# A two-layer transformer trunk on one core: the third gate/up chunk takes its K pairs in the later chunks' order, and a hold on two weight rests is taken out

## The chip, the cores and the metric

The kernel runs on one core of one Trainium2 chip. The metric is device time in microseconds (us), less is better. Before the change three runs took 2182.69, 2183.49 and 2186.39; the median is 2183.49.

## What is computed

Two layers, 256 tokens, model width 2048, feed-forward width 5632, all in float32:

```python
def reference(x, ...):
    for l in range(DEPTH):                                  # DEPTH = 2
        h = rms_norm(x, pre_mix_norm[l])
        m = hybrid_mixer(h, l, w_in[l], w_o[l], ...)        # two kinds of attention
        x = x + rms_norm(m, post_mix_norm[l])
        h = rms_norm(x, pre_ffn_norm[l])
        f = swiglu(h, w_gate[l], w_up[l], w_down[l])
        x = x + rms_norm(f, post_ffn_norm[l])
    return x

def swiglu(h, w_gate, w_up, w_down):
    return (jax.nn.silu(h @ w_gate) * (h @ w_up)) @ w_down
```

The change touches `h @ w_gate` and `h @ w_up` alone.

## The kernel before

**Products in three.** Each float32 weight tile is split in two: `hi` is a rounded copy that ScalarE (ACT) makes (L310), and `lo`, the rest, is the tile minus `hi`, mostly made by VectorE (DVE, L320), in a few cases by GpSimd (POOL, L313). The tokens are split likewise. A product is then three matmuls on TensorE (PE): hi x hi, hi x lo, lo x hi.

**Chunks and pairs.** The gate/up phase of a layer has 11 chunks of 512 columns, c = 0 to 10. A chunk takes the 2048 rows of K in 8 pairs of 256, kp = 0 to 7. Each pair brings two tiles of 128 x 1024 values: one of `w_gate`, one of `w_up`. Tiles are numbered in the order in which the program takes them, and names carry these numbers. In layer 1, pair (1, 6) is tiles 156 and 157, (1, 7) is 158 and 159, (2, 0) is 160 and 161. The next two pairs of chunk 2 are 162 to 165. Later (3, 5) is 186 and 187, (3, 6) is 188 and 189, (3, 7) is 190 and 191, and (4, 0) is 192 and 193.

**Plain and seven-product pairs.** A plain pair (`eight`, matmuls at L1255) is 24 matmuls. A seven-product pair forms seven products in place of eight blocks (Strassen's way), 21 matmuls (`seven_products`, its three at L1137, L1138 and L1139). It needs sums of weight blocks. The up tile, called T, comes with a second DMA by POOL that adds the gate tile's first half on the way (L259); the gate tile is called G. `mixed_weights` then has DVE subtract within T (L291), add that to G (L292), and form three rests behind ACT's copies (L280, L282): `lo`, `Tl` of 512 values, `Tl` of 1024 values. PE wants these in the order lo, Tl 512, Tl 1024. Token sums for it are made once in chunks 0 to 2 (`pair_sums`).

Chunk 1 has seven-product pairs kp = 5 and 6; chunk 2 has 2, 4, 5 and 6; chunks 3 to 9 (`MORE_AT`) have 2, 3, 4, 5 and 6. Chunk 2 takes its pairs as 0, 1, 2, ... 7; chunks 3 to 9 take them as 0, 2, 1, 3, ... 7 (`MORE_ORDER`), so that a seven-product pair is second.

**Buffers.** The plain tiles (`raw`) have 4 buffers, `hi` 6, `lo` 6, G 3, T 4. Weights lie in DRAM in the order of use. SyncE (SP) issues their loads in one queue, first in, first out (raw L242, G L231, T L258): a load whose buffer isn't free yet holds up all that stand behind it.

**Who sets the order.** Most instructions are placed by a scheduler in the compiler that goes by its own times and by dependencies that the program adds. Three of those matter here. After a chunk's last seven-product pair DVE adds up the shared products (`shared_part`, L1179 to L1182). If the next chunk's second pair is a seven-product pair, that pair's rests are made to come behind these (`follows`); if not, the next plain rest that the program asks for is held behind them (`held`). And the POOL's rest of the second pair's gate tile waits for the newest seven-product matmul (`helped`). Finally `last_of_row` names the up tile of pair (1, 6) in each layer: the two plain rests that come after it, those of pair (1, 7), are held behind its last Tl.

**A chunk's end.** With the last pair the chunk before last is transposed on PE (L1372), and ACT copies the result out of PSUM (L1373), two copies; the next chunk's sums go into the banks that they free. DVE and ACT then drain the finished chunk's banks (L1433 to L1439), and its seven-product pairs' banks are in turn those of the next chunk but one.

Of the kernel before, what the change touches and what calls it, by code (L numbers as in the profile page):

```python
# [45 lines left out]
NEXT_SEVEN = (5, 6)  # L46
MORE_SEVEN = (2, 3, 4, 5, 6)
MORE_AT = (3, 4, 5, 6, 7, 8, 9)
# [24 lines left out]

def gate_order(c):

    if c in MORE_AT:
        return MORE_ORDER
    return FIRST_ORDER if c == 0 else tuple(range(KT // 2))


def weight_order():

    order = []

    def queue_pair(name, l, kp, c):
        order.append((name, l, kp, c))
        return len(order) - 1

    plan = []
    sevens, plain, own = set(), set(), set()  # L90
    for l in range(L):
        lay = {"in": {}, "o": {}, "gate": {}, "up": {}, "down": {}}
        for n, (ca, cb) in enumerate(PAIRS):
            for kp in IN_ORDER if n else range(KT // 2):
                lay["in"][ca, kp] = queue_pair("w_in", l, kp, ca)
                lay["in"][cb, kp] = queue_pair("w_in", l, kp, cb)
                if kp in IN_NOW[n]:
                    plain.add(lay["in"][cb, kp])
        order_o = [(c, kp) for kp in KP_O for c in (0, 1)]
        order_o += [(c, kp) for kp in LATE_O for c in (2, 3)] + [(c, kp) for c in (2, 3) for kp in LAST_O]  # L100
        lay["order_o"] = order_o
        for c, kp in order_o:
            lay["o"][c, kp] = queue_pair("w_o", l, kp, c)
            if c == 3 and kp in O_SEVEN:
                own.add(lay["o"][c, kp])
        for c in range(FF // CW):
            for kp in gate_order(c):
                lay["gate"][c, kp] = queue_pair("w_gate", l, kp, c)
                lay["up"][c, kp] = queue_pair("w_up", l, kp, c)
                if kp in gate_sevens(c):  # L110
                    sevens.add(lay["up"][c, kp])
        for half in range(2):
            for kp in range(FF // P // 2):
                for c in (2 * half, 2 * half + 1):
                    lay["down"][c, kp] = queue_pair("w_down", l, kp, c)
                if kp in DOWN_SEVEN[half]:
                    sevens.add(lay["down"][2 * half + 1, kp])
        plan.append(lay)
    return order, plan, sevens, plain, own
# [48 lines left out]
def kernel(  # L168
# [35 lines left out]
    order, plan, sevens, plain, own = weight_order()  # L204
# [3 lines left out]
    for lay in plan:  # L208
        for c in range(1, FF // CW):
            for n in (1, 2):  # L210
                helped[lay["gate"][c, gate_order(c)[n]]] = n == 1
    newest_seven = [None]
    last_of_row = {lay["up"][1, NEXT_SEVEN[-1]] for lay in plan}

    ready = {}
    raws, loads = [], []
# [47 lines left out]
    def mixed_weights(i):  # L264

        g, u = raws[i - 1], raws[i]
        hi = wpool.tile([P, 2, CW], F32R, tag="hi", bufs=6, name=f"hi{i}")
        lo = wpool.tile([P, 2, CW], F32R, tag="lo", bufs=6, name=f"lo{i}")
        if i in own:
            th = wpool.tile([P, 2, CW], F32R, tag="hi", bufs=6, name=f"Th{i}")  # L270
            tl = wpool.tile([P, 2, CW], F32R, tag="lo", bufs=6, name=f"Tl{i}")
            th2 = mix_pool[0].tile([P, 2 * (S + P)], F32R, tag="ah", bufs=1, name=f"T2h{i}")[:, 0:CW]
            tl2 = mix_pool[0].tile([P, 2 * (S + P)], F32R, tag="al", bufs=1, name=f"T2l{i}")[:, 0:CW]
        else:
            th = mix_pool[0].tile([P, 3, CW], F32R, tag="Th", bufs=1 if i in plain else 2, name=f"Th{i}")
            tl = mix_pool[0].tile([P, 3, CW], F32R, tag="Tl", bufs=1 if i in plain else 2, name=f"Tl{i}")
            th2, tl2 = th[:, 2, :], tl[:, 2, :]

        def split(h, l, w):
            nc.scalar.activation(h, w, AF.Copy)  # L280
            with in_row(i):
                newest_rest[i] = nc.vector.tensor_tensor(out=l, in0=w, in1=h.bitcast(F32), op=ALU.subtract)  # L282

        if i in plain or i in own:
            with after_rests():
                nc.vector.tensor_tensor(out=u[:, 0, :], in0=g[:, 0, :], in1=u[:, 0, :], op=ALU.add)
        split(hi, lo, u)
        t1, b22 = ((hi[:, k, :], lo[:, k, :]) for k in range(2))
        t3, t4 = ((th[:, k, :], tl[:, k, :]) for k in range(2))
        t2 = u[:, 1, :]  # L290
        nc.vector.tensor_tensor(out=t2, in0=t2, in1=u[:, 0, :], op=ALU.subtract)  # L291
        nc.vector.tensor_tensor(out=g, in0=g, in1=t2.unsqueeze(1).to_broadcast([P, 2, CW]), op=ALU.add)  # L292
        split(th2, tl2, t2)
        split(th[:, 0:2, :], tl[:, 0:2, :], g)
        if i in last_of_row:
            held[:] = newest_rest[i], 2
        t2 = th2, tl2
        return {"b22": b22, "t1": t1, "t2": t2, "t3": t3, "t4": t4}

    def feed(upto):  # L300
        fetch(upto)
        while fed[0] < min(upto, len(stream)):
            i = fed[0]
            raw = raws[i]
            if i in sevens or i in plain or i in own:
                ready[i] = mixed_weights(i)
                fed[0] += 1
                continue
            hi = wpool.tile([P, 2, CW], F32R, tag="hi", bufs=6, name=f"hi{i}")
            nc.scalar.activation(hi, raw, AF.Copy)  # L310
            lo = wpool.tile([P, 2, CW], F32R, tag="lo", bufs=6, name=f"lo{i}")
            if i in helped:
                rest = nc.gpsimd.tensor_tensor(out=lo, in0=raw, in1=hi.bitcast(F32), op=ALU.subtract)  # L313
                if helped[i]:
                    tc.add_manual_dep(rest.ins, newest_seven[0].ins.name, AFTER, reason="the shared port")
                ready[i] = (hi, lo)
                fed[0] += 1
                continue
            with behind():
                rest = nc.vector.tensor_tensor(out=lo, in0=raw, in1=hi.bitcast(F32), op=ALU.subtract)  # L320
            ready[i] = (hi, lo)
            fed[0] += 1
            rests.append(rest)
# [21 lines left out]
    held = [None, 0]  # L345
    follows, newest_rest = {}, {}

    def in_row(i):

        return tc.issue_after(follows[i].ins) if i in follows else nullcontext()  # L350
# [8 lines left out]
    def after_rests():  # L359

        return tc.issue_after(rests[-1].ins)
# [826 lines left out]
    for l in range(L):  # L1188
# [27 lines left out]
        for kp in LATE_O[:-1]:  # L1216
            i, j = (plan[l]["o"][c, kp] for c in (2, 3))
# [44 lines left out]
        with tc.manual_schedule(engines=by_hand):  # L1262
# [35 lines left out]
            fetch(fed[0] + 4)  # L1298
            first_banks = four_banks(1, [f"c{q}_{l}_0" for q in ("11", "12", "21", "22")])
            first, second, third, fourth = gate_order(0)[:4]  # L1300
            eight(first_banks, 0, first, (0,), True, False, ahead=0)
            eight(first_banks, 0, second, (0,), False, False, (0,), 0)
# [302 lines left out]
```

## Time and profile before

| | |
|---|---|
| runs, us | 2182.69, 2183.49, 2186.39 (median 2183.49) |
| profiled execution | 2185.51 us, span 2183.8 |
| PE busy | 2168.2 us, 99% |
| DVE busy | 1912.0 us, 88% |
| ACT busy | 1392.1 us, 64% |
| POOL busy | 256.1 us, 12% |
| PE's clock | full in all slices |
| weights from DRAM | 215 GB/s over the span |
| gate/up chunk 2, layer 1 | 482.88 to 527.32 us |
| gate/up chunks 3 to 9, layer 1 | 527.32 to 815.96 us |
| the same in layer 2 | 1569.90 to 1612.32, and to 1902.80 us |

Times in rows of a time line are from the start of the span: start, length, engine, line, operation, tile written <- tiles read, shape; in brackets how long the engine was idle before it and what ended that. Consecutive rows of one kind are merged (x4 is four of them). In the waits view the numbers behind the colon are us in total, times, and the longest.

### The profile page before, as it was taken

To read this page: it belongs to the slowest core of one execution; us is meant where nothing else is said; L and a number is where in the kernel's file an instruction comes from. 1 tells how busy PE (TensorE), PEld (TensorE's weight loads), DVE (VectorE), ACT (ScalarE), POOL (GpSimd) and SP (SyncE) were. 2 spreads that over 40 slices of the span, in tenths; PEclk is the share of its full clock that TensorE was granted. 3 is DMA by queue.
4 is the path that set the end of the run, shared out by engine and by line. 5 is a ranking of instruction groups with operands and counts; after the bars stand their busy time and mean duration, and the time that the engine had idled before them with its cause. 6 is when DMAs were issued, how large, how long until landed. Compare 5 with 4: busy or idle time off the path is not lost.

```text
span 2183.8 us, 28775 instructions
## 1 busy us (share of the span) xinstructions
PE 2168.2 (99%) x9956; PEld 1783.6 (82%) x9956; DVE 1912.0 (88%) x2641; ACT 1392.1 (64%) x2081; POOL 256.1 (12%) x239
## 2 busy tenths in 40 slices
PE   9999999999999999999999999999999999999998
PEld 7888888887888888888878888888888888888886
DVE  7888658889999999999878886588899999999997
ACT  7666665756666666666665666657566666576664
POOL 2100000021222220000010000000222222200000
PEclk9999999999999999999999999999999999999999
DMA  9545555488887777767465555545888877767683
GB/s 336 182 163 174 193 185 177 155 281 247 242 257 229 231 231 236 234 227 254 147 241 174 175 176 186 193 158 179 285 244 237 260 221 230 237 228 242 207 266 100
DMA packets 140274, 470.43 MB, mean 215 GB/s; under 512 B 15952, under 2 KB 16976, under 8 KB 139616
## 3 DMA queue, kind: packets, MB, share of 16 engines
q1 hardware_dynamic: 121952, 436.03, 57.8%
q0 software_dynamic: 17600, 32.02, 8.9%
q8 instruction: 78, 1.28, 0.2%
q10 hardware_dynamic: 576, 0.54, 0.1%
q14 instruction: 68, 0.56, 0.1%
HBM read 460.14 MB, written 8.39 MB: 215 GB/s over the span
## 4 chain that ended last, share of the span: by engine, by line
PE 80%; DVE 11%; issue 3%; DMA 3%; ACT 2%; DVEq 0%; ACTq 0%
PE c L1255 15%; PE in L1137 6%; PE in L1139 6%; PE in L1138 6%; PE dn L1486 4%; PE dn L1487 4%; PE dn L1489 4%; DVE lo L320 3%; PE o L609 2%; PE o L611 2%; PE o L610 2%; DVE Tl L282 2%; PE p L1138 2%; PE c L1138 2%; PE c L1137 2%
## 5 line engine op out<-in xcount | busy, mean ns | idle before, releaser
L320 DVE TENSOR_TENSOR lo<-raw,hi 128x1024 fp32r<-128x1024 f32 x464 | 557.7, 1224 | 105.8 <-ACT hi L310 104.8
L310 ACT ACTIVATE hi<-raw 128x1024 fp32r<-128x1024 f32 x486 | 496.2, 1053 | 86.4 <-DMA raw<-in_weights_in_turn_dram 38.3
L1255 PE MATMUL c<-hi,xF 128*128 128x512 f32 x1344 | 364.0, 392 | 0.9 <-DVE xF L519 0.5
L1255 PEld LDWEIGHTS c<-hi,xF 128*128 128x128 f32 x1344 | 250.2, 188 | 52.6 <-DVE xF L519 1.3
L259 POOL DMA_DIRECT2D T<-in_weights_in_turn_dram x122 | 107.6, 882 | 1394.8 <-PE c L1255 545.2
L1255 PE MATMUL c<-lo,xF 128*128 128x512 f32 x672 | 207.3, 390 | 0.0
L280 ACT ACTIVATE Th<-G 128x1024 fp32r<-128x1024 f32 x122 | 128.8, 1056 | 76.6 <-DVE G L292 75.3
L1486 PE MATMUL dn<-hi,jh 128*128 128x512 f32 x416 | 162.0, 389 | 0.0
L1487 PE MATMUL dn<-lo,jh 128*128 128x512 f32 x416 | 161.8, 389 | 0.0
L280 ACT ACTIVATE Th<-T 128x512 fp32r<-128x512 f32 x122 | 77.2, 633 | 130.2 <-DVE T L291 127.3
L282 DVE TENSOR_TENSOR Tl<-G,Th 128x1024 fp32r<-128x1024 f32 x122 | 149.2, 1223 | 11.3 <-ACT Th L280 11.3
L282 DVE TENSOR_TENSOR lo<-T,hi 128x1024 fp32r<-128x1024 f32 x122 | 155.3, 1273 | 0.7 <-ACT hi L280 0.6
L310 ACT ACTIVATE hi<-G 128x1024 fp32r<-128x1024 f32 x122 | 128.4, 1052 | 36.1 <-DMA G<-in_weights_in_turn_dram 34.5
L292 DVE TENSOR_TENSOR G<-G,T 128x1024 f32<-128x1024 f32 x122 | 148.9, 1221 | 1.8
L1255 PEld LDWEIGHTS c<-lo,xF 128*128 128x128 f32 x672 | 126.0, 188 | 26.3
L320 DVE TENSOR_TENSOR lo<-G,hi 128x1024 fp32r<-128x1024 f32 x104 | 127.0, 1221 | 11.8 <-ACT hi L310 11.7
L280 ACT ACTIVATE hi<-T 128x1024 fp32r<-128x1024 f32 x122 | 128.0, 1049 | 13.3 <-PE c L1139 10.3
L1137 PE MATMUL in<-hi,xT 128*128 128x512 f32 x328 | 131.0, 401 | 0.7 <-ACT hi L942 0.7
L1137 PE MATMUL in<-hi,xI 128*128 128x512 f32 x328 | 131.2, 401 | 0.0
L1138 PE MATMUL in<-lo,xI 128*128 128x512 f32 x328 | 128.0, 390 | 0.3 <-DVE lo L320 0.3
L1489 PE MATMUL dn<-hi,jl 128*128 128x512 f32 x416 | 128.1, 389 | 0.0
L1139 PE MATMUL in<-hi,xI 128*128 128x512 f32 x328 | 128.0, 391 | 0.0
(487 smaller groups left out, 4925.9 us busy)
## 6 DMA issues: line engine op xcount, KB each, us to landing
raw<-in_weights_in_turn_dram SPq DMA_DIRECT2D x498, 512.0 KB, 4.7
T<-in_weights_in_turn_dram SPq DMA_DIRECT2D x122, 512.0 KB, 5.5
G<-in_weights_in_turn_dram SPq DMA_DIRECT2D x122, 512.0 KB, 5.6
T<-in_weights_in_turn_dram POOLq DMA_DIRECT2D x122, 256.0 KB, 5.9
GU<-in_weights_in_turn_dram SPq DMA_DIRECT2D x32, 512.0 KB, 6.5
V<-in_weights_in_turn_dram SPq DMA_DIRECT2D x8, 512.0 KB, 3.8
away_ffn<-x SPq DMA_DIRECT2D x8, 512.0 KB, 8.4
xd<-away_ffn SPq DMA_DIRECT2D x8, 512.0 KB, 8.7
```

The costliest lines, as they stand in the source:

```text
L280: nc.scalar.activation(h, w, AF.Copy)
L282: newest_rest[i] = nc.vector.tensor_tensor(out=l, in0=w, in1=h.bitcast(F32), op=ALU.subtract)
L292: nc.vector.tensor_tensor(out=g, in0=g, in1=t2.unsqueeze(1).to_broadcast([P, 2, CW]), op=ALU.add)
L310: nc.scalar.activation(hi, raw, AF.Copy)
L320: rest = nc.vector.tensor_tensor(out=lo, in0=raw, in1=hi.bitcast(F32), op=ALU.subtract)
L1137: nc.tensor.matmul(a, sh, hi, start=first, stop=False, skip_group_check=open_sums[0])
L1138: nc.tensor.matmul(a, sh, lo, start=False, stop=False, skip_group_check=open_sums[0])
L1139: return nc.tensor.matmul(a, sl, hi, start=False, stop=last, skip_group_check=open_sums[0])
L1255: nc.tensor.matmul(a, stat[part], w[j][:, kk, :], start=first and kk + n == 0, stop=last and kk == 1 and n == 2)
L1486: nc.tensor.matmul(accs[c, t], sh, hi[:, kk, :], start=first, stop=False, skip_group_check=open_sums[0])
L1487: nc.tensor.matmul(accs[c, t], sh, lo[:, kk, :], start=False, stop=False, skip_group_check=open_sums[0])
L1489: nc.tensor.matmul(accs[c, t], sl, hi[:, kk, :], start=False, stop=last, skip_group_check=open_sums[0])
```

## The change

Two edits. `gate_order` gives chunk 2 the order of chunks 3 to 9, so that its seven-product pair kp = 2 is second: in layer 1 it becomes tiles 162 and 163, and plain pair kp = 1 tiles 164 and 165. The weights in DRAM are laid out in that order too, and `follows` takes the place of `held` at the end of chunk 1. And `last_of_row` and its hold go. Both hold for both layers. The tables of which pairs are seven-product pairs are the same, and so is the count of matmuls.

```diff
 def gate_order(c):
-    if c in MORE_AT:
+    if c in MORE_AT or c == MORE_AT[0] - 1:
         return MORE_ORDER
     return FIRST_ORDER if c == 0 else tuple(range(KT // 2))
...
-    last_of_row = {lay["up"][1, NEXT_SEVEN[-1]] for lay in plan}
...
         split(th[:, 0:2, :], tl[:, 0:2, :], g)
-        if i in last_of_row:
-            held[:] = newest_rest[i], 2
```

In the changed file the lines behind the edits are numbered lower, by 1 from L214 on and by 3 from L297 on: L242 is L241, L282 is L281, L320 is L317, L1179 is L1176, L1373 is L1370.

The edits move instructions on several engines. The first place is DVE's queue at the end of chunk 1 in layer 1, before:

```order
L282 TENSOR_TENSOR Tl157_4430<-T157_4334,Th157_4429 128x512
L282 TENSOR_TENSOR Tl157_4430<-G156_4421,Th157_4429 128x1024
L320 TENSOR_TENSOR lo158_4471<-raw158_4467,hi158_4469 128x1024
L320 TENSOR_TENSOR lo159_4477<-raw159_4473,hi159_4475 128x1024
L320 TENSOR_TENSOR lo160_4504<-raw160_4500,hi160_4502 128x1024
L320 TENSOR_TENSOR lo161_4513<-raw161_4509,hi161_4511 128x1024
L1179 TENSOR_TENSOR w1_0_1_4537<-p6_0_1_4464,w0_0_1_4536 128x512
L1180 TENSOR_TENSOR w2_0_1_4538<-p7_0_1_4465,w1_0_1_4537 128x512
L1181 TENSOR_TENSOR w1_0_1_4537<-q5_0_1_4466,w1_0_1_4537 128x512
L1182 TENSOR_TENSOR w3_0_1_4539<-q5_0_1_4466,w2_0_1_4538 128x512
L320 TENSOR_TENSOR lo163_4555<-raw163_4551,hi163_4553 128x1024
L1433 TENSOR_TENSOR w0_0_1_4536<-c11_0_1_4237,w0_0_1_4536 128x512
```

And after (the first rows, then those behind L1179, which is what L1182 was):

```order
L281 TENSOR_TENSOR Tl157_4430<-T157_4334,Th157_4429 128x512
L317 TENSOR_TENSOR lo158_4471<-raw158_4467,hi158_4469 128x1024
L281 TENSOR_TENSOR Tl157_4430<-G156_4421,Th157_4429 128x1024
L317 TENSOR_TENSOR lo159_4480<-raw159_4476,hi159_4478 128x1024
...
L1179 TENSOR_TENSOR w3_0_1_4539<-q5_0_1_4466,w2_0_1_4538 128x512
L281 TENSOR_TENSOR lo163_4552<-T163_4473,hi163_4551 128x1024
L290 TENSOR_TENSOR T163_4473<-T163_4473 128x512
L291 TENSOR_TENSOR G162_4545<-G162_4545,T163_4473 128x1024
L281 TENSOR_TENSOR Tl163_4554<-T163_4473,Th163_4553 128x512
L281 TENSOR_TENSOR Tl163_4554<-G162_4545,Th163_4553 128x1024
L1430 TENSOR_TENSOR w0_0_1_4536<-c11_0_1_4237,w0_0_1_4536 128x512
```

The plain rest lo158 now stands between the two Tl of pair (1, 6), and the second pair's rests and sums, five instructions, stand ahead of the draining of chunk 1.

The second place is SP's queue of loads around there, before:

```order
L242 DMA raw158_4467<-in_weights_in_turn_dram 128x1024
L242 DMA raw159_4473<-in_weights_in_turn_dram 128x1024
L242 DMA raw160_4500<-in_weights_in_turn_dram 128x1024
L258 DMA T165_4506<-in_weights_in_turn_dram 128x1024
L242 DMA raw161_4509<-in_weights_in_turn_dram 128x1024
L231 DMA G164_4606<-in_weights_in_turn_dram 128x1024
L242 DMA raw162_4545<-in_weights_in_turn_dram 128x1024
L242 DMA raw163_4551<-in_weights_in_turn_dram 128x1024
```

And after:

```order
L241 DMA raw158_4467<-in_weights_in_turn_dram 128x1024
L257 DMA T163_4473<-in_weights_in_turn_dram 128x1024
L241 DMA raw159_4476<-in_weights_in_turn_dram 128x1024
L241 DMA raw160_4503<-in_weights_in_turn_dram 128x1024
L241 DMA raw161_4509<-in_weights_in_turn_dram 128x1024
L230 DMA G162_4545<-in_weights_in_turn_dram 128x1024
L257 DMA T169_4618<-in_weights_in_turn_dram 128x1024
L230 DMA G168_4693<-in_weights_in_turn_dram 128x1024
L241 DMA raw164_4612<-in_weights_in_turn_dram 128x1024
```

The second pair's tiles are loaded as T163 and G162 ahead of the next two raw tiles, not as raw162 and raw163 behind them.

The third place is DVE's queue at the end of chunk 3 (pairs (3, 5), (3, 6) and (3, 7)), before:

```order
L282 TENSOR_TENSOR Tl187_5118<-T187_5028,Th187_5117 128x512
L291 TENSOR_TENSOR T189_5070<-T189_5070 128x512
L282 TENSOR_TENSOR Tl187_5118<-G186_5109,Th187_5117 128x1024
L292 TENSOR_TENSOR G188_5148<-G188_5148,T189_5070 128x1024
L282 TENSOR_TENSOR Tl189_5157<-T189_5070,Th189_5156 128x512
L320 TENSOR_TENSOR lo190_5191<-raw190_5187,hi190_5189 128x1024
L282 TENSOR_TENSOR Tl189_5157<-G188_5148,Th189_5156 128x1024
L320 TENSOR_TENSOR lo191_5200<-raw191_5196,hi191_5198 128x1024
```

And after:

```order
L281 TENSOR_TENSOR Tl187_5118<-T187_5028,Th187_5117 128x512
L290 TENSOR_TENSOR T189_5070<-T189_5070 128x512
L317 TENSOR_TENSOR lo190_5191<-raw190_5187,hi190_5189 128x1024
L281 TENSOR_TENSOR Tl187_5118<-G186_5109,Th187_5117 128x1024
L291 TENSOR_TENSOR G188_5148<-G188_5148,T189_5070 128x1024
L281 TENSOR_TENSOR Tl189_5157<-T189_5070,Th189_5156 128x512
L317 TENSOR_TENSOR lo191_5200<-raw191_5196,hi191_5198 128x1024
L281 TENSOR_TENSOR Tl189_5157<-G188_5148,Th189_5156 128x1024
```

Each of the two plain rests lo190 and lo191 stands three places further forward, ahead of a Tl of 1024. The same holds for chunks 2 and 4 to 9 and in layer 2, though their code is not edited. On ACT, in chunks 2 to 9, the two copies L1373 (now L1370) each move behind one more copy of Th.

## The prediction

> **What bounds the kernel now.** I read the busy shares first, then what TensorE (PE) waits for, then the time line around the third gate/up chunk. Pairs are written (chunk, K pair); layer 1 is the first.
>
> ```profile
> PE 2168.2 (99%) x9956; PEld 1783.6 (82%) x9956; DVE 1912.0 (88%) x2641; ACT 1392.1 (64%) x2081; POOL 256.1 (12%) x239
> PE p L1138 <- DVE Tl L282: 2.7, 4, 1.3
> PE c L1255 <- ACT act L1373: 0.5, 1, 0.5
> ```
>
> PE is busy for 99% of the span, and the number of matmuls doesn't change, so only the rest can be won. The waits that the view books are small, but matmuls overlap (0.39 us each, started 0.227 apart), so a short stall is hidden inside a "busy" row. I therefore go by starts:
>
> ```profile
> 482.88 0.39 PE L1255 MATMUL c<-hi,xF 128*128 128x512 f32 x1
> 483.73 0.96 PE L1255 MATMUL c<-hi,xF 128*128 128x512 f32 x3 [0.45 <-ACT act L1373]
> ...
> 516.96 0.39 PE L1137 MATMUL p<-Th,sh 128*128 128x512 f32 x1
> 517.44 0.50 PE L1138 MATMUL p<-Tl,sh 128*128 128x512 f32 x1
> ...
> 518.01 0.42 PE L1137 MATMUL p<-Th,sh 128*128 128x512 f32 x1
> 519.71 0.50 PE L1138 MATMUL p<-Tl,sh 128*128 128x512 f32 x1 [1.28 <-DVE Tl L282]
> ...
> 523.70 1.07 PE L1255 MATMUL c<-hi,xF 128*128 128x512 f32 x4
> ...
> 525.06 1.04 PE L1372 MATMUL actT_ps<-ident,act 128*128 128x128 f32 x8
> ...
> 527.32 1.07 PE L1255 MATMUL c<-hi,xF 128*128 128x512 f32 x4
> ```
>
> Six matmuls (four and two) take 1.36, from 523.70 to the transposes at 525.06, so 0.227 each. At the start of chunk 2 the second matmul comes 0.85 after the first: 0.62 lost, and about 0.1 more at the second copy (L1373), 0.72 in all. In the chunk's last seven-product pair the rests Tl come late: 517.44 - 516.96 is 0.48 (0.25 lost), 519.71 - 518.01 is 1.70 (1.47 lost), and with a few slow starts beside them about 1.94.
>
> A chunk of 3 to 9 has 3 plain pairs of 24 matmuls and 5 of 21, 177 in all: 177 x 0.227 = 40.1, and the eight transposes 0.9 (525.06 to 527.32 is 2.26, less six matmuls). So PE alone needs about 41.05. Chunk 2 has 180 matmuls: 41.7.
>
> ```profile
> 482.88:527.32 44.44, 42.61 (x189) 34.39 (x188) 43.51 (x50) 26.37 (x33) 11.39 (x9) 1.00 0.92 291
> 527.32:815.96 288.64, 288.56 (x1296) 237.81 (x1295) 279.02 (x308) 188.50 (x218) 66.32 (x47) 1.00 0.78 234
> 1569.90:1612.32 42.42, 42.04 (x190) 34.54 (x189) 41.84 (x49) 25.13 (x30) 10.88 (x9) 1.00 0.91 292
> 1612.32:1902.80 290.48, 289.14 (x1296) 237.68 (x1295) 279.76 (x310) 188.84 (x219) 67.21 (x47) 1.00 0.77 232
> ```
>
> The columns are the length, then busy time of PE, PE's weight loads, DVE, ACT and POOL, then clock (full), DMA share and GB/s. Against the PE-only lengths, chunk 2 loses 44.44 - 41.7 = 2.7 in layer 1 and 0.7 in layer 2; chunks 3 to 9 lose 288.64 - 7 x 41.05 = 1.3 and 290.48 - 287.35 = 3.1. All that the change could possibly remove is 7.8 us, 0.36%. And DVE has 279.0 busy us of 288.6 there: it is nearly a second bound.
>
> **The change part by part.** (a) Chunk 1's last two plain rests lose their hold. Before, DVE, ACT and SP did this at the boundary of layer 1:
>
> ```profile
> 471.29 1.23 DVE L282 TENSOR_TENSOR Tl<-G,Th 128x1024 fp32r<-128x1024 f32 x1 [0.73 <-ACT Th L280]
> 472.43 4.62 DVE L320 TENSOR_TENSOR lo<-raw,hi 128x1024 fp32r<-128x1024 f32 x4
> 476.97 0.69 DVE L1179 TENSOR_TENSOR w<-p,w 128x512 f32<-128x512 f32 x1
> ...
> 479.09 0.68 DVE L1182 TENSOR_TENSOR w<-q,w 128x512 f32<-128x512 f32 x1
> 483.23 1.23 DVE L320 TENSOR_TENSOR lo<-raw,hi 128x1024 fp32r<-128x1024 f32 x1 [3.46 <-ACT hi L310]
> ...
> 488.36 3.63 DVE L282 TENSOR_TENSOR lo<-T,hi 128x1024 fp32r<-128x1024 f32 x1 [0.19 <-ACT hi L280]
> 482.14 1.06 ACT L310 ACTIVATE hi<-raw 128x1024 fp32r<-128x1024 f32 x1 [3.66 <-DMA raw<-in_weights_in_turn_dram]
> 483.11 1.05 ACT L1373 COPY act<-actT_ps 128x512 f32<-128x512 f32 x2
> 456.63 0.42 SPq L231 DMA_DIRECT2D G<-in_weights_in_turn_dram  x1
> 473.73 1.77 SPq L242 DMA_DIRECT2D raw<-in_weights_in_turn_dram  x2
> 488.20 2.71 POOL L313 TENSOR_TENSOR lo<-G,hi 128x1024 fp32r<-128x1024 f32 x1
> ```
>
> lo158 and lo159 are the first two of the four rests at 472.43 (4.62 / 4 = 1.15 each, 1.13 from start to start). SP issued nothing from 456.63 to 473.73: it stood at a load into a raw buffer that such a rest frees, and every later load stood behind it. That is why raw163 is late, ACT copies hi163 only at 482.14, DVE idles 3.46, and the two L1373 copies, queued behind hi163 on ACT, end at 484.16, after PE wants the banks. In the new order lo158 stands ahead of the last Tl, and fits into the 0.73 idle with about 0.3 left over: L1179 comes 0.8 earlier, at about 476.1.
>
> (b) Chunk 2's second pair is now a seven-product pair: hi163 comes from T163, whose load is issued ahead of raw159 and blocked by no rest, so hi163 is ready long before L1182 is done, at about 478.9. The 3.46 idle goes. On ACT the first L1373 stands behind one small Th copy only. Chunk 4 shows what it then waits for:
>
> ```profile
> 566.22 1.04 PE L1372 MATMUL actT_ps<-ident,act 128*128 128x128 f32 x8
> 566.86 0.59 ACT L1373 COPY act<-actT_ps 128x512 f32<-128x512 f32 x1 [5.46 <-PE actT_ps L1372]
> 532.66 1.40 DVE L1439 SCALAR_TENSOR_TENSOR act<-c,rs_ffn,w 128x512 f32<-128x512 f32 x2
> ```
>
> It ends 0.64 + 0.59 after the transposes start. At chunk 2 these start at 482.88 - 2.26 = 480.6, so it ends at 481.9, before PE wants it at 483.1. The 0.72 goes. The second L1373 is now behind Th163's long copy (1.06): about 483.7, wanted at 484.2; cover 0.5, and if it is gone the cost is that excess, at every chunk start.
>
> (c) Five more operations (lo163 to Tl163, 4.6) stand ahead of L1433 to L1439, which drain the banks that the seven-product pair writes. In chunk 3, which has this order already, the drain (last row above) ends at 534.06, 12.2 after L1179 (521.84, below). Here that is 488.4, and the third product wants its bank at 482.88 + 5.45 + 1.36 = 489.7. Covered by 1.3.
>
> (d) Chunk 2's end.
>
> ```profile
> 517.29 1.22 DVE L320 TENSOR_TENSOR lo<-raw,hi 128x1024 fp32r<-128x1024 f32 x1
> 518.43 1.22 DVE L282 TENSOR_TENSOR Tl<-G,Th 128x1024 fp32r<-128x1024 f32 x1
> 519.57 2.36 DVE L320 TENSOR_TENSOR lo<-raw,hi 128x1024 fp32r<-128x1024 f32 x2
> 521.84 0.69 DVE L1179 TENSOR_TENSOR w<-p,w 128x512 f32<-128x512 f32 x1
> ```
>
> From lo163 (483.23) to the end of the last Tl (519.65) DVE needed 36.4 without idling much. Now it starts at 478.9, and one more plain rest (lo176, 1.13) stands ahead of that Tl: 516.5. DVE will wait for some buffers that PE frees, since it now runs further ahead: 0.4 to 1.0. So 516.9 to 517.5, where PE, without the 0.72, wants it at 517.15. Stall 0 to 0.4, I take 0.2 instead of 1.94. Chunk 2 gains 0.72 + 1.74 = 2.5 in layer 1.
>
> (e) Chunks 3 to 9 are not edited, but each now has one more plain rest ahead of the second last seven-product pair's last Tl.
>
> ```profile
> 543.32 1.05 ACT L310 ACTIVATE hi<-G 128x1024 fp32r<-128x1024 f32 x1
> 545.48 1.22 DVE L320 TENSOR_TENSOR lo<-G,hi 128x1024 fp32r<-128x1024 f32 x1
> ...
> 549.48 1.23 DVE L320 TENSOR_TENSOR lo<-G,hi 128x1024 fp32r<-128x1024 f32 x1 [0.52 <-ACT hi L310]
> ...
> 554.71 1.23 DVE L282 TENSOR_TENSOR Tl<-G,Th 128x1024 fp32r<-128x1024 f32 x1
> ```
>
> The last of these rows is that Tl; it ended at 555.94. PE reaches it 127 matmuls behind the chunk's start, 527.32 + 28.8 = 556.1. Slack 0.2, with L1179 5.48 ahead of the chunk (521.84 against 527.32). With 1.13 more in front, the lead must be about 6.4. After (d) it is: L1179 at 518.4, chunk 3 at 527.32 - 2.5 = 524.86, so 6.46. The lead won in chunk 2 is thus just spent on the added rest, and no stall is new at chunk 3. After that DVE's own period decides. Of layer 1 the chunks took 288.64 / 7 = 41.23, PE-bound 41.05; I see no DVE work or wait removed, so they lose about the same 1.3 again, plus 0.2 for the slack that is gone.
>
> (f) Layer 2.
>
> ```profile
> 1563.87 2.40 POOL L313 TENSOR_TENSOR lo<-raw,hi 128x1024 fp32r<-128x1024 f32 x1 [13.38 <-PE c L1139]
> 1568.51 1.23 DVE L320 TENSOR_TENSOR lo<-raw,hi 128x1024 fp32r<-128x1024 f32 x1 [3.22 <-ACT hi L310]
> ```
>
> Here DVE idled 3.22 and would start lo163 at 1565.3, while POOL's lo162 runs to 1566.3 (it waits for PE, so it doesn't move). The nearest row is the collision in layer 1: POOL from 488.20, DVE's rest at 488.36 took 3.63 instead of 1.22 and ended 1.1 after POOL did. By that row lo163 is 1.0 late, and with it the copies L1373 up to 0.35, so I book +0.35 at chunk 2's start. Only 0.7 was lost in chunk 2, of which I take 0.6 as won, and chunks 3 to 9 stay: -0.25 in all, from +1.0 (nothing won, the copies late, the rest's slack gone) to -0.7.
>
> The Trainium skill (SBUF — State Buffer, "Who interferes with whom") says that a DVE instruction with two SBUF inputs contends with a GpSimd instruction that reads SBUF, and that the first to issue blocks the other fully. The 3.63 agrees; it speaks against moving a second-pair rest under POOL's, and gives the same 1.0.
>
> **Sum.** -2.5 + 0.2 - 0.25 = -2.55, say -2.5. The profiled execution took 2185.51 (span 2183.8 and 1.7 around it), so 2183.0; it lies 2.0 above the median of the runs, 2183.49. Against the median: 2181.0. Own range of this case: stalls 0 to 0.4 in (d), (e) 0 to 0.4, (f) +1.0 to -0.7, and 0.3 for stalls read from starts: -1.0 to -4.2, 2179.3 to 2182.5.
>
> **The rivals.** A measurement of this kernel tells about 0.2%, 4.4 us, from no change.
>
> R1, the lead stays. DVE keeps not 6.4 but 1 to 2 us more, since G and T loads are issued earlier throughout chunk 2 and the added rest fills time in which DVE would wait for a copy (0.52 at 549.48). Then chunks 3 to 9 lose little of their 1.3 and 3.1: up to -2.5 - 4.4 - 0.6, so -4.5 to -7.5; I take -6.0, 2177.5. For it: DVE's busy time, 279.0 / 7 = 39.9 a chunk, is below PE's 41.05. Against: DVE's waits in those chunks come from loads and copies that depend on DVE itself, and the period was 41.23 with the old order.
>
> R2, no lead comes. DVE, done early with (1,7), waits for buffers that PE frees, and the lost 1.94 returns elsewhere; the added rest costs 1.13 per layer: 2.26 - 0.72 and the late second copies 0 to 1.8. That is 0 to +3.3; I take +1.0, 2184.5.
>
> R3, slower. The place is the last Tl of (c,5) in all 14 chunks of 3 to 9. Loop: PE ends the third pair 24 + 21 + 24 = 69 matmuls into the chunk (527.32 + 15.7 = 543.0) and frees a weight buffer; ACT copies into it (543.32 to 544.37), DVE takes the rest up at 545.48, after 1.1 of slack, and comes to the end of Tl at 555.94: 12.9, 11.8 without the slack. With the added rest it is 12.9 again, against PE's 556.1 - 543.0 = 13.1. It decides once the wait at 549.48, for a G load, grows by over 0.2 above its 0.52. Then no lead helps: each chunk pays anew, the rest's 1.13 less up to half of it for cover: 0.6 to 1.1, 8 to 15 in all, less 2.5 to 3.4 from chunk 2: +5 to +12, I take +8, 2191.5. For it: slack of 0.2 on a path with a DMA in it. Against: SP's order of those G loads is as before up to chunk 3.
>
> That the orders don't change is excluded: the instruction streams show it.
>
> **How the numbers follow.** Forecast 0.36, R1 0.28, R2 0.12, R3 0.24. The forecast and R2 lie within 4.4. I give 0.03 of the forecast to faster (its lower end is at the bound): faster 0.31, same 0.33 + 0.12 = 0.45, slower 0.24. Range: 2177.0 cuts off a fifth of R1 (0.06), 2190.0 over half of R3 (0.14): 0.2 left out.
>
> **What would show it.** Right: SP issuing between 456 and 473, no idle of 3 us on DVE ahead of the second pair's rest, no PE wait at L1370 (the old L1373), the last Tl of chunk 2 in time, chunk 2 at about 42 in layer 1, and chunks 3 to 9 at 288.5 and 290.5 again. R1: those below 288 and 289. R2: chunk 2 still near 44. R3: a PE wait for Tl (L281 now) of 0.5 or more in each chunk at (c,5), with 41.8 or more a chunk. The forecast is wrong if the stretches of 3 to 9 move by more than 2 us.

## The result and the profile after

18 runs of the changed kernel had a median of 2180.53 us (2178.97 to 2182.41), 18 of the kernel before 2184.36 (2182.25 to 2186.91). The ratio is 0.9983, 95% interval 0.9977 to 0.999: 3.7 us faster, within 0.2% and inside the range that was forecast. The forecast had been 2.5 us. The profiled execution after took 2180.98 us, span 2179.3, so 4.5 less than the one before.

The busy line of the whole execution after, and PE's waits from 482 to 1899 us, which holds chunks 2 to 9 of both layers:

```profile
PE 2167.0 (99%) x9956; PEld 1783.9 (82%) x9956; DVE 1913.4 (88%) x2641; ACT 1395.5 (64%) x2081; POOL 246.3 (11%) x239
PE p L1135 <- DVE Tl L281: 0.5, 3, 0.2
PE c L1252 <- ACT act L1370: 0.2, 1, 0.2
```

2.7 and 0.5 us of booked waits became 0.5 and 0.2. The table by stages, after: chunk 2 and chunks 3 to 9 of layer 1, then of layer 2 (length, then busy time of PE, weight loads, DVE, ACT, POOL):

```profile
482.56:525.22 42.66, 42.31 (x189) 34.47 (x188) 41.27 (x49) 25.89 (x31) 10.00 (x8) 1.00 0.87 269
525.22:813.74 288.52, 288.25 (x1296) 237.97 (x1295) 279.09 (x309) 190.22 (x219) 62.86 (x48) 1.00 0.79 235
1567.46:1609.63 42.17, 42.02 (x189) 34.54 (x188) 40.79 (x48) 25.40 (x31) 9.99 (x8) 1.00 0.88 269
1609.63:1898.30 288.67, 288.67 (x1297) 237.79 (x1296) 278.60 (x309) 190.14 (x219) 62.74 (x48) 1.00 0.78 234
```

Against before: -1.78 (44.44), -0.12 (288.64), -0.25 (42.42) and -1.81 (290.48), together -4.0 of the 4.5 between the two spans.

DVE at the boundary of layer 1, after. L1176 is what L1179 was, L1179 what L1182 was:

```profile
470.96 1.22 DVE L317 TENSOR_TENSOR lo<-raw,hi 128x1024 fp32r<-128x1024 f32 x1
472.10 1.22 DVE L281 TENSOR_TENSOR Tl<-G,Th 128x1024 fp32r<-128x1024 f32 x1
473.24 3.49 DVE L317 TENSOR_TENSOR lo<-raw,hi 128x1024 fp32r<-128x1024 f32 x3
476.64 0.68 DVE L1176 TENSOR_TENSOR w<-p,w 128x512 f32<-128x512 f32 x1
...
478.76 0.68 DVE L1179 TENSOR_TENSOR w<-q,w 128x512 f32<-128x512 f32 x1
479.36 1.21 DVE L281 TENSOR_TENSOR lo<-T,hi 128x1024 fp32r<-128x1024 f32 x1
...
488.60 3.09 DVE L317 TENSOR_TENSOR lo<-raw,hi 128x1024 fp32r<-128x1024 f32 x1
```

lo158 fills the place of the 0.73 idle, and lo163 follows L1179 at once: the 3.46 idle is gone. SP, which before issued nothing from 456.63 to 473.73, now stands from 457.66 to 467.36:

```profile
457.66 0.38 SPq L257 DMA_DIRECT2D T<-in_weights_in_turn_dram  x1
467.36 0.33 SPq L230 DMA_DIRECT2D G<-in_weights_in_turn_dram  x1
```

What is left late on PE, with the copies on ACT:

```profile
481.87 0.57 ACT L1370 COPY act<-actT_ps 128x512 f32<-128x512 f32 x1
482.65 1.06 ACT L279 ACTIVATE Th<-G 128x1024 fp32r<-128x1024 f32 x1 [0.21 <-DVE G L291]
483.62 0.56 ACT L1370 COPY act<-actT_ps 128x512 f32<-128x512 f32 x1
484.23 0.73 PE L1252 MATMUL c<-hi,xF 128*128 128x512 f32 x2 [0.16 <-ACT act L1370]
517.03 0.39 PE L1134 MATMUL p<-Th,sh 128*128 128x512 f32 x1
517.61 0.50 PE L1135 MATMUL p<-Tl,sh 128*128 128x512 f32 x1 [0.19 <-DVE Tl L281]
```

The second copy waits behind Th163, which waits for DVE's sum of G162. The copy ends at 484.18; PE, which began the chunk at 482.56, was ready six matmuls later, at 483.92. It starts 0.32 late and loses 0.11 more behind that: 0.43 in all. At the chunk's end Tl173 is 0.46 late (517.61 - 517.03 less 0.227 is 0.35, and 0.11 behind it), where the rests Tl of that pair cost 1.94 before.

The main reading is DVE's own time. From L1179 (after: L1176) of chunk 1 to that of chunk 9, in layers 1 and 2, before and then after (length, DVE busy):

```profile
476.97:810.76 333.79, 321.06 (x357) 1.00 0.80 240
1562.47:1897.69 335.22, 320.70 (x355) 1.00 0.79 240
```

```profile
476.64:807.53 330.89, 320.91 (x357) 1.00 0.80 239
1560.45:1892.01 331.56, 320.99 (x356) 1.00 0.79 239
```

DVE does the same 321 us of work; its idle time fell from 12.7 and 14.5 to 10.0 and 10.6. DVE thus wins 2.9 and 3.7 us.

Not all of that reaches PE. Call the time from this sum of DVE to the start of the next chunk on PE the lead. PE took 1.9 and 2.1 us; the lead at the start of chunk 10 grew by 1.0 and 1.2 (from 5.2 and 5.1 to 6.2 and 6.3), and in layer 2 the lead at the start of chunk 2 was 0.4 smaller than before, which is the rest. The grown lead isn't spare. Before, the lead was 5.5 at chunk 3 and came down to 5.1, never further; after, it was 6.6 and came down to 6.2, never further. There PE waits for Tl, and the 1.1 between the two values is what the added rest needs, as step (e) of the prediction said.

### The profile page after: what moved, and what is told of

It is laid out like the page before. It is cut to its first block, busy times and chain, and to the rows that moved or that the text cites. A ratio compares the mean times of both kernels' runs of the same rounds, so it can differ in the third digit from the quotient of the medians.

```text
span 2179.3 us, 28774 instructions
## 1 busy us (share of the span) xinstructions
PE 2167.0 (99%) x9956; PEld 1783.9 (82%) x9956; DVE 1913.4 (88%) x2641; ACT 1395.5 (64%) x2081; POOL 246.3 (11%) x239
## 3 DMA queue, kind: packets, MB, share of 16 engines
q8 instruction: 78, 1.28, 0.2%
## 4 chain that ended last, share of the span: by engine, by line
PE 91%; DVE 5%; issue 2%; ACT 1%; DMA 1%; DVEq 0%; SPq 0%; ACTq 0%
PE c L1252 19%; PE in L1134 7%; PE in L1136 6%; PE in L1135 6%; PE dn L1484 4%; PE dn L1483 4%; PE dn L1486 4%; PE p L1135 3%; PE c L1134 2%; PE p L1136 2%; PE c L1135 2%; PE c L1136 2%; PE p L1134 2%; PE o L606 2%; PE o L608 2%; PE o L607 2%
## 5 line engine op out<-in xcount | busy, mean ns | idle before, releaser
L317 DVE TENSOR_TENSOR lo<-raw,hi 128x1024 fp32r<-128x1024 f32 x464 | 561.6, 1229 | 100.0 <-ACT hi L307 98.9
L281 DVE TENSOR_TENSOR Tl<-G,Th 128x1024 fp32r<-128x1024 f32 x122 | 148.9, 1221 | 11.6 <-ACT Th L279 11.6
L281 DVE TENSOR_TENSOR lo<-T,hi 128x1024 fp32r<-128x1024 f32 x122 | 153.1, 1255 | 0.1
L317 DVE TENSOR_TENSOR lo<-G,hi 128x1024 fp32r<-128x1024 f32 x104 | 126.8, 1219 | 10.2 <-ACT hi L307 10.2
```

## The experiments

### Each edit alone

```diff
 # e1_order_only, against before: the order of chunk 2, the hold stays
-    if c in MORE_AT:
+    if c in MORE_AT or c == MORE_AT[0] - 1:
 # e2_hold_only, against before: the hold goes, the order stays
-    last_of_row = {lay["up"][1, NEXT_SEVEN[-1]] for lay in plan}
...
-        if i in last_of_row:
-            held[:] = newest_rest[i], 2
```

Expected of the order alone: 

> The order edit alone; the hold on the last two rests of (1, 7) stays. Theory: the order edit carries the change, and the hold's part is the 0.8 us of lead that lo158 wins by filling the idle ahead of the last Tl of (1, 6). Without it L1176 at the end of chunk 1 comes at about 477.4 and not 476.64, the last Tl of chunk 2 and of (3, 5) are late by up to 0.8 more: 0.5 to 1.6 us slower than with both edits, so 2.1 to 3.2 us faster than before. Rival, the order does all: as with both edits, 3.7 us faster, within 0.4. Rival, the hold does most: at most 1.5 us faster than before.

Measured: a median of 2180.80 (11 runs) against 2183.55 for the kernel before (27 runs), ratio 0.9991 (0.9982 to 1.0): 2.0 us faster, with an interval (0 to 3.9) that takes in the theory and both rivals. Its profile, chunk 2's start and the four stages:

```profile
483.97 0.40 PE L1255 MATMUL c<-hi,xF 128*128 128x512 f32 x1
484.84 0.96 PE L1255 MATMUL c<-hi,xF 128*128 128x512 f32 x3 [0.47 <-ACT act L1373]
...
486.58 0.50 PE L1255 MATMUL c<-hi,xF 128*128 128x512 f32 x1 [0.33 <-ACT act L1373]
483.97:527.57 43.60, 42.58 (x190) 34.38 (x189) 42.22 (x49) 26.69 (x33) 9.99 (x8) 1.00 0.89 284
527.57:815.49 287.92, 287.92 (x1297) 237.92 (x1296) 278.78 (x309) 190.43 (x219) 62.71 (x48) 1.00 0.78 235
1569.09:1611.19 42.10, 42.04 (x190) 34.54 (x188) 40.72 (x48) 25.43 (x31) 9.99 (x8) 1.00 0.87 277
1611.19:1898.83 287.64, 287.64 (x1297) 237.99 (x1296) 278.69 (x309) 190.57 (x219) 63.07 (x48) 1.00 0.78 235
```

With the hold left in, both copies are late and chunk 2 of layer 1 takes 43.60, 0.9 more than with both edits. But chunks 3 to 9 take 0.6 and 1.0 less, so the four stages together lose nothing (661.3 against 662.0, and 666.0 before). They have the added rest ahead of Tl just the same. The lead at chunk 3 is 6.6 here too: DVE goes on while PE waits at the start of chunk 2, so that this wait is made up for later.

Expected of the hold alone: 

> The hold alone is taken out; chunk 2 keeps its old order. On the engines only lo158 and the last Tl of (1, 6) change places, and a few loads on SP. Theory: lo158 and lo159 come 0.7 us earlier, raw163's load with them, so the stall at chunk 2's start in layer 1 (0.72) goes and that at its end (1.94) shrinks to about 1.2: 1.0 to 1.9 us faster than before, DVE still idle for about 3 us ahead of lo163. Rival, the idle only grows: no change, within 0.4. Rival, the hold does most: over 2.2 us faster.

Measured: 2181.15 (11 runs), ratio 0.9989 (0.998 to 0.9998), 2.4 us faster: by the number the hold does most, but the interval (0.4 to 4.4) leaves only "no change" out. DVE ahead of lo163, PE at Tl173, and chunk 2 of both layers (the four stages together take 662.5):

```profile
482.03 1.23 DVE L317 TENSOR_TENSOR lo<-raw,hi 128x1024 fp32r<-128x1024 f32 x1 [1.27 <-ACT hi L307]
518.23 0.50 PE L1135 MATMUL p<-Tl,sh 128*128 128x512 f32 x1 [0.72 <-DVE Tl L281]
483.10:525.86 42.76, 42.04 (x190) 34.55 (x188) 42.18 (x50) 25.11 (x30) 11.38 (x9) 1.00 0.92 296
1568.73:1610.49 41.76, 41.76 (x190) 34.59 (x188) 41.33 (x47) 24.72 (x30) 10.45 (x8) 1.00 0.90 279
```

The idle is 1.27, and not 3 as I had counted. Part of that is the load of raw163, whose landing differs between executions: in the second profile of before the same idle was 2.11, with no edit at all. So the two edits remove the same wait: the order all of it (in e1 lo163 follows L1182 at once), the hold 0.8 to 2.2 us of it. In the stages their gains, 4.7 and 3.5, don't add up, since both together have 4.0. The run times can't show that: their intervals don't separate e1, e2 and both edits.

### The added rest in chunks 2 to 9

```diff
 # e3_old_rows, against after
+    wait_for = {}
+    for lay in plan:
+        wait_for[lay["gate"][3, 0]] = lay["up"][2, 6]
+        for c in MORE_AT:
+            wait_for[lay["gate"][c, 7]] = lay["up"][c, 5]
+            wait_for[lay["up"][c, 7]] = lay["up"][c, 6]
...
-            with behind():
+            with tc.issue_after(newest_rest[wait_for[i]].ins) if i in wait_for else behind():
```

The two rests are put back behind the Tl that they stood behind before the change.

> Both edits, but the plain rests in the rows of chunks 2 to 9 are put back behind the Tl that they stood behind before (lo176 behind Tl173, lo190 behind Tl187, lo191 behind Tl189 and so on); ACT and SP then have their old order in these chunks too, and PE's is the same in all kernels. Theory, the added rest uses up the lead that chunk 2 wins: the Tl of (2, 6), 0.46 late in layer 1 and 0.42 in layer 2, and those of (c, 5), 0.2 to 0.4 late in seven chunks, are in time: 1.5 to 3 us faster than with both edits, 5.2 to 6.7 faster than before. Rival, DVE's own period sets chunks 3 to 9, so the lead is used up by their end either way: 0.3 to 1.2 faster than with both edits. Rival, the new row order helps (it puts a copy and a rest where ACT and DVE would idle): slower than with both edits by 0.5 to 3.

Measured: 2180.31 (11 runs), ratio 0.9984 (0.9975 to 0.9993), as with both edits (0.9983). Stages:

```profile
483.14:524.85 41.71, 41.71 (x189) 34.63 (x188) 39.80 (x47) 25.04 (x31) 10.10 (x8) 1.00 0.85 267
524.85:813.01 288.16, 288.16 (x1296) 238.08 (x1295) 279.27 (x310) 188.97 (x219) 65.45 (x47) 1.00 0.75 232
1566.56:1608.82 42.26, 42.05 (x190) 34.52 (x188) 40.35 (x47) 24.80 (x30) 10.48 (x8) 1.00 0.86 273
1608.82:1898.13 289.31, 288.98 (x1297) 237.80 (x1295) 278.90 (x308) 188.58 (x218) 66.82 (x47) 1.00 0.75 232
```

Chunk 2 of layer 1 loses nothing any more (41.7 is PE alone), 0.95 better than with both edits; chunks 3 to 9 of layer 2 are 0.6 worse. The sum of the four, 661.4, lies between the two profiles of both edits (662.0, and 661.0 in e9 below). My theory fell (1.5 to 3 us expected), and by the number the first rival (0.3 to 1.2) does no better, though the interval of about 2 us to either side leaves it in. The rows say why nothing is won: without the added rest the lead at chunk 3 is only 5.9 and 5.5, not 6.6, and comes down to 5.1, not 6.2. PE needs 1.1 less of lead, and DVE has about as much less.

### Is DVE the bound?

```diff
 # against after, for the up tile of (c, 1) in chunks 3 to 9
 # e5_rest_twice: its rest is made twice
+    some = {lay["up"][c, 1] for lay in plan for c in MORE_AT}
...
+            if i in some:
                 rest = nc.vector.tensor_tensor(out=lo, in0=raw, in1=hi.bitcast(F32), op=ALU.subtract)
 # e6_rest_less: its rest isn't made
+            if i in some:
+                ready[i] = (hi, hi)
+                fed[0] += 1
+                continue
```

e6 leaves a part of the product out: the rounded copy stands in the place of the rest. The matmuls are as many as before, so it measures DVE's share of the time and is no kernel to use.

> Both edits; in chunks 3 to 9 of both layers DVE makes one plain rest (the up tile of (c, 1)) twice, 14 instructions of 1.13 us more. Theory, DVE's own row of work sets these chunks (41.2 us a chunk from one L1176 to the next, PE alone 41.05): its period becomes 42.3, chunks 3 to 9 take 7 to 9 us longer in each layer, 13 to 17 us in all, about 2195. Rival, PE binds and DVE only waits for it and for loads (its 0.8 us of idle a chunk takes the rest up): at most 3 us more. Rival, the row order alone makes the stalls: with the rest early in the chunk, no change.

> Both edits; in chunks 3 to 9 of both layers one plain rest (the up tile of (c, 1)) is left out, and the matmuls take the rounded copy in its place: the part of the sum that this rest brings is wrong, DVE has 14 instructions of 1.13 us less, all else is as it was. Theory, DVE's own row sets these chunks: PE then binds, chunks 3 to 9 take 287.4 to 287.8 us in place of 288.5 and 288.7, the kernel is 1.5 to 2.5 us faster than with both edits. Rival, DVE waits for buffers or loads and the 1.13 us only become idle time: within 0.6 us of both edits.

Twice: 2216.41 (4 runs), ratio 1.0145 (1.0129 to 1.0161), 32 us slower. Once less: 2177.93 (11 runs), ratio 0.9975 (0.9966 to 0.9984), 5.5 us faster than before; that is 2.6 below the median with both edits, which ran beside other runs of before, and 1.7 by the two ratios. Chunks 3 to 9, of both layers in e5, then of layer 1 in e6 (layer 2 takes 287.22 too):

```profile
524.79:828.57 303.78, 292.10 (x1289) 237.79 (x1288) 295.27 (x311) 183.50 (x215) 62.03 (x46) 0.99 0.72 219
1625.51:1931.53 306.02, 293.94 (x1289) 239.07 (x1288) 292.72 (x311) 184.22 (x216) 62.49 (x46) 0.98 0.71 216
```

```profile
524.73:811.95 287.22, 287.22 (x1296) 238.37 (x1295) 273.58 (x302) 190.23 (x219) 63.58 (x48) 1.00 0.78 237
```

e6 settles the floor: 287.22 is 41.03 a chunk, PE alone. With 1.13 us a chunk less on DVE its lead stays between 6.5 and 7.1, above the 6.2, and PE never waits there. e5 is the other side, and twice as dear as the theory said (13 to 17 us): DVE is busy 16.2 and 14.1 us more, where 7 rests are 7.9. Most of the difference comes from places like this, in DVE, POOL and PE rows:

```profile
649.87 5.79 DVE L291 TENSOR_TENSOR T<-T 128x512 f32<-128x512 f32 x1
649.99 2.76 POOL L311 TENSOR_TENSOR lo<-G,hi 128x1024 fp32r<-128x1024 f32 x1
652.36 2.74 POOL L311 TENSOR_TENSOR lo<-raw,hi 128x1024 fp32r<-128x1024 f32 x1
660.50 0.79 PE L1137 MATMUL p<-hi,xF 128*128 128x512 f32 x1 [4.80 <-DVE w L1433]
```

DVE, late by then, meets both of POOL's rests; a sum of 0.69 takes 5.79, and PE waits 4.80 for the banks that DVE drains behind it. In that place, being late makes DVE later still. PE's clock adds to it: behind this wait it was granted 0.50 from 660.5 to 664 and 0.79 to 668, which by these shares is about 2.6 us of work lost (my estimate). The 32 us are thus not DVE's two rests alone.

### The collision in chunk 2

```diff
 # e7_no_help, against after
-                helped[lay["gate"][c, gate_order(c)[n]]] = n == 1
+                if (c, n) != (2, 2):
+                    helped[lay["gate"][c, gate_order(c)[n]]] = n == 1
 # e8_old_rows_no_help: the same on e3_old_rows;  e11_hold_only_no_help: on e2_hold_only
```

> Both edits, but in chunk 2 of both layers the third pair's gate rest (lo164 and its like in layer 2) is made by DVE and not by POOL. With both edits POOL's 2.7 us for it ran beside DVE's lo165, which took 3.09 us in layer 1 and 3.19 in layer 2 in place of 1.22. Theory, the collision costs DVE more than the help saves: DVE is 0.7 us earlier at the end of chunk 2 in each layer (L1176 at 517.9 and not 518.61), Tl of (2, 6) nearly in time: 0.5 to 1.5 us faster than with both edits. Rival, DVE waits there for buffers that PE frees, so the collision is hidden: slower by 0 to 2.

Measured: 2179.29 (11 runs), ratio 0.9981 (0.9973 to 0.999): 1.2 below the median with both edits, but by the two ratios 0.4, so the gain isn't clear of noise. What the rows show is clear: DVE makes four rests in 4.62 us, where three took 5.36 with both edits (first row), and chunk 2 takes PE's own 41.71 in both layers (layer 1 shown):

```profile
488.60 5.36 DVE L317 TENSOR_TENSOR lo<-raw,hi 128x1024 fp32r<-128x1024 f32 x3
488.60 4.62 DVE L318 TENSOR_TENSOR lo<-raw,hi 128x1024 fp32r<-128x1024 f32 x4
483.11:524.82 41.71, 41.71 (x189) 34.62 (x188) 40.33 (x49) 25.66 (x31) 7.64 (x7) 1.00 0.85 263
```

> The kernel with both edits and the old rows in chunks 2 to 9, with the third pair's rest of chunk 2 moved to DVE as well. Theory, DVE's 0.7 us per layer and the rows' 0.5 to 1 us add up: 0.5 to 1.5 us faster than the old rows alone, 4.5 to 6 faster than before. Rival, both only move lead about that chunks 3 to 9 use up: within 0.5 of the old rows alone.

Measured: 2178.45 (11 runs), ratio 0.9976 (0.9968 to 0.9985): 5.2 faster than before. It was 1.9 below e3, and 1.7 by the ratios, a little more than the 1.5 expected; the rival, within 0.5, isn't excluded by the intervals. Chunks 3 to 9 of both layers:

```profile
525.33:812.58 287.25, 287.25 (x1296) 238.35 (x1295) 278.58 (x309) 188.98 (x218) 63.26 (x47) 1.00 0.76 233
1607.86:1895.06 287.20, 287.20 (x1297) 238.36 (x1295) 278.06 (x308) 189.08 (x217) 63.54 (x47) 1.00 0.76 234
```

This is PE alone again, with all of DVE's work done: the lead is 6.4 at chunk 3 of both layers, where PE needs 5.1 in this order, and still 5.8 and 6.1 at chunk 10.

> The hold is out, chunk 2 keeps its old order, and the third pair's rest of chunk 2 is made by DVE and not by POOL. Theory, DVE's time from chunk 1 to 9 decides, however it is saved: the collision (2.1 us of excess in layer 1, 3.0 in layer 2, less 1.1 for the rest that DVE now makes) goes, 1 to 2 us faster than the hold alone, as fast as both edits with no help or up to 1 us slower. Rival, the order edit is needed for it: no faster than the hold alone, within 0.6.

Measured: 2179.25 (11 runs), ratio 0.9983 (0.9974 to 0.9992), 3.7 faster than before; 1.9 below e2 in the medians (1.3 by the ratios), and 0.9 above the kernel of e8 on the same chip. So without the order edit, too, most of the gain is to be had, if the hold goes and DVE makes that rest.

### Both kernels once more

> The kernel before once more, for a second profile of it. In the first one, chunks 4 and 5 of layer 2 lost 1.1 and 0.9 us on Tl, after DVE had waited 1.8 us for a G tile's load. Theory, one late load in one execution: no stall over 0.5 us there, chunks 3 to 9 of layer 2 take 288.5 to 289.2 us and not 290.5. Rival, the order of before makes that load late each time: 290 to 291 again, with the stalls at the same pairs.

One run of before, 2187.21. Chunk 2 of layer 1, and chunks 2 and 3 to 9 of layer 2:

```profile
482.90:528.33 45.43, 43.95 (x189) 35.60 (x188) 44.30 (x51) 26.67 (x33) 10.93 (x9) 0.96 0.92 299
1570.69:1614.89 44.20, 42.48 (x189) 34.39 (x188) 43.62 (x50) 25.76 (x32) 11.33 (x9) 1.00 0.91 299
1614.89:1904.52 289.63, 289.15 (x1297) 237.78 (x1296) 279.73 (x310) 188.94 (x220) 67.28 (x47) 1.00 0.77 233
```

Neither answer: 289.63 lies between the two, with smaller stalls at the same pairs, and chunk 2 of layer 2 lost 2.5 us in place of 0.7. In layer 2 the loss of before moves between stages from one execution to the next; its sum is 332.9 and 333.8. With both edits that sum was 330.8, and 330.0 in e9. The gain of 1.8 in chunks 3 to 9 and 0.25 in chunk 2 is therefore best read together, as 2 to 4 us.

> Both edits once more, for a second profile and as the measure for the two kernels that run with it. 3 to 4.5 us faster than before; chunk 2 of layer 1 between 42.3 and 43, chunks 3 to 9 of both layers 288.3 to 289.2.

> The kernel with both edits, the old rows in chunks 2 to 9, and the third pair's rest of chunk 2 on DVE, beside both edits on the same chip. Its profile had next to no stall on PE in chunks 2 to 9 (41.03 to 41.07 a chunk). Theory: 1.5 to 2.5 us faster than both edits. Rival, the two profiles differ by chance: within 0.8.

On one chip: both edits 2180.06 (ratio 0.9988, 0.9979 to 0.9997), the kernel of e8 2178.33 (ratio 0.998, 0.9971 to 0.9989), 11 runs each. Both edits missed what I expected of them: 2.6 us faster by the ratio, not 3 to 4.5. The stages took 42.13, 288.86, 41.71 and 288.29, the first and the last a little below the expected ranges. The means of the two kernels differ by 1.55, and from the spread of the 22 runs I work out 0.9 as the 95% uncertainty of that. e8's kernel is thus faster than both edits, by how much is open (0.6 to 2.5, which takes in the theory and the rival's 0.8). Nor does it reach the floor each time: chunks 3 to 9 took 287.19 and 288.04, and in layer 2 the lead had come down to 5.1.

## Why the prediction was right, point by point

The time of the likeliest case was 2181.0, measured 2180.53. That this is so near is luck in part: the gain was forecast as 2.5 us and measured as 3.7, the stages were off in both directions, and the median of before was 2184.36 in 18 runs, 0.9 above that of the three from which I counted. What held was the mechanism in layer 1; in layer 2 the gain came from a term that I had put at next to nothing. By its steps:

- (a) and (b): L1179 of chunk 1 at 476.1 forecast, 476.64 measured; lo163 at 478.9, measured 479.36; the idle gone, as said. The first copy ended at 482.44 for 481.9. The second was mis-sized: I let it be done at 483.7 for a need of 484.2. It only started at 483.62, behind a copy that waited for DVE, and ended at 484.18; and PE, which began the chunk 0.32 earlier than in the first profile, needed it at 483.92. 0.43 was lost where I had nought.
- (d): Tl173 forecast for 516.9 to 517.5 and 0.2 late; done at 517.55 and 0.46 late. Chunk 2 gained 1.8 in place of 2.5. In e9 it took 42.13, a gain of 2.3.
- (e): 1.5 us lost in chunks 3 to 9 of layer 1 forecast, 288.52 - 287.35 = 1.2 measured. The lead was used up as said: 6.46 forecast at chunk 3 for a need of 6.4, measured 6.6 and 6.2. e6 bears out that what is lost behind that is set by DVE. That the added rest costs PE its 1.13 as a loss of its own isn't borne out: in e3, without it, nothing was won.
- (f) was the wrong step: it left layer 2's chunks 3 to 9 at their 3.1 us lost. They lost 1.3, in e9 0.9. I treated DVE's 3.22 idle ahead of lo163 as worth only chunk 2's own 0.6, though (e) had just said that DVE sets the later chunks; DVE's stretch in layer 2 became 3.7 shorter, and the lead at chunk 3 rose from 5.5 to 6.6. That term, -0.25, measured -2.1, in e9 -2.9. Part of it is that the 3.1 came from one execution: the second profile of before lost 2.3 there and 2.5 in chunk 2. The collision there was half of what was forecast, 0.5 and not 1.0, since POOL began 0.97 behind L1176 (1560.45) and not 1.4:

```profile
1563.16 1.73 DVE L281 TENSOR_TENSOR lo<-T,hi 128x1024 fp32r<-128x1024 f32 x1
1561.42 2.40 POOL L310 TENSOR_TENSOR lo<-G,hi 128x1024 fp32r<-128x1024 f32 x1 [6.54 <-PE c L1136]
```

- So -2.5 had two errors that partly cancel: 0.4 too much in layer 1 (-2.3 for -1.9), 1.8 too little in layer 2 (-0.25 for -2.1).

R1 was in part what happened in layer 2. R2 fell: the lead came. (Its lower end didn't follow from its terms, either: 2.26 - 0.72 is 1.5, not 0.) R3 fell with every stage: chunks 3 to 9 didn't lengthen, though (c, 5) kept stalls of 0.1 to 0.4 in some chunks.

Of the signs named for the forecast, the end of the 3 us idle, SP issuing between 456 and 473 and the 288.5 of layer 1 came. A booked wait of 0.2 at L1370, Tl 0.46 late, 42.66 for "about 42" and 288.67 in layer 2 for "290.5 again" did not. The sign against it, a move of chunks 3 to 9 by more than 2 us, was all but met: 1.8 in layer 2, and 2.2 by the profile of e9.

## What to carry to other kernels

Where a second engine's work is within a few per cent of the bound's, follow its lead over the whole stretch and not only the stalls of the bound: an idle of 3 us taken away at one boundary was paid out over the chunks behind it, until the lead had come down to where the bound waits. The idle that was saved, 2.9 and 3.7 us, gives the direction and an upper end; the bound got 1.9 and 2.1. Two edits that remove the same wait needn't add. And a helper engine that takes 1.1 us of work off the second bound can be a loss if its 2.7 us block that engine: here 1.9 us of delay for 1.1 saved. Of the three pairs of kernels that differ in this alone, all point that way (by the ratios 0.4, 1.7 and 1.3 us), but in each pair the intervals overlap.

## What the runs showed of the hardware

DVE blocked by POOL was not let in between two POOL instructions. In e5 a sum of 0.69 stood against two rests of POOL, 2.76 and 2.74 back to back; it ended 0.6 behind the second one, 5.79 in all. The Trainium skill (SBUF — State Buffer, "Who interferes with whom") says that a DVE instruction with two SBUF inputs contends with a GpSimd instruction that reads SBUF, and that issue order decides who blocks. The prediction's row agrees: POOL from 488.20, DVE's rest at 488.36, done 1.1 behind POOL. In e5 the rows don't show it: the sum starts 0.12 before POOL's first rest, though behind a load issue of POOL at 649.43. Of a second instruction that follows, the section says nothing.

PE's clock fell behind a short wait in one execution. In the second profile of before, this stretch of chunk 2 of layer 1 has PE idle for 1.07 of 2 us, and the granted clock is 0.50 behind it (third number from the end):

```profile
518.00:520.00 2.00, 0.93 (x4) 0.80 (x5) 2.00 (x2) 1.61 (x2) 0.00 (x0) 0.98 0.65 125
520.00:522.00 2.00, 2.00 (x7) 1.52 (x6) 1.90 (x4) 0.00 (x0) 0.89 (x1) 0.50 0.96 320
```

Matmuls started 0.43 apart, and about 1 us was lost on top of the wait. The first profile had the same wait there (1.28), and the second one had it again in layer 2 (1.28 at 1607.24), both at full clock throughout. The Trainium skill (TensorE: Matmul & The Clock Gate, "Why this matters for your kernels") asks for no idle gaps of over about 3 us. Here the clock fell behind gaps of 0.35 and 1.5 us, in one of three such places. What picks the one wasn't tried.
